# The low parts of all weight blocks: a negated copy on ScalarE and an accumulating DMA in place of a VectorE subtract

## The chip, the cores and the metric

The kernel runs on one core of a Trainium2 chip. The metric is device time in microseconds. Engines are named as the profile names them: PE is TensorE's matrix multiply and PEld its weight load, DVE is VectorE, ACT is ScalarE, POOL is GpSimd, SP is SyncE, which issues DMAs. Each engine works through a queue of its own in order; a semaphore holds an instruction back until what it needs is there, and everything behind it in that queue waits too.

## The reference

Four layers of width 1024 over 1024 positions, with the token mixers convolution, state space, RWKV-7 and convolution again. All is float32. Cut to what matters:

```python
for i in range(DEPTH):                      # DEPTH = 4
    kind, j = i % N_MIXERS, i // N_MIXERS   # 0 conv, 1 S5, 2 RWKV-7
    ...                                     # y = mixer(x), its products with conv_w_in, ssm_w_in, rwkv_w_rkvz, ..._w_out
    r = DN_ALPHA * x + y
    r = r + (p[i] @ ple_proj[i]) * jax.nn.sigmoid(r @ ple_gate[i])
    x = layer_norm(r, ln_g[i], ln_b[i])
```

The convolution's mixer is `(bg * conv * silu(z)) @ w_out` with `bg, cg, h, z` the four quarters of `x @ w_in`. Nearly all arithmetic is in products of activations with weight matrices.

## The kernel before

**Products from hi and lo parts.** A float32 product is made of three products of operands in a second format, fp32r. Every operand is split: hi is the value rounded to fp32r, lo is the value less hi. `mm3` (L317) adds hi x hi (L326), hi weight x lo activation (L327) and lo weight x hi activation (L328) in PSUM. So each block of weights is needed as two tiles, `wh` and `wl`.

**Blocks of weights.** A block is 128 columns of a matrix, held as 128 partitions x 8 x 128 values (512 KB). `wload` (L290) loads it into a raw tile `wraw` by a DMA of SyncE (L295), rounds it into `wh` on ScalarE (L298) and writes `wl = wraw - wh` on VectorE (L299). Each of the three tiles has three buffers, and `w_fill` loads two blocks ahead (AHEAD = 2) of the one in use, in the order of `weight_order`. So the split of a block can begin only when TensorE has finished with the block that held its buffers, and must be done when TensorE comes to it. A block of one 512-column half is used by 24 products (8 depths x 3); in some stages both halves use it, 48 products.

**Stages.** In the gate stages (`gate_half`, L908) each of eight blocks of `ple_gate` is used by 24 products (tile `gp`), followed by 6 products with a block of `ple_proj` (tile `pp`), which stays for four of them and holds one of the three buffers meanwhile. GpSimd sums r (L920) and the row sums for the layer norm (`ln_s`, L905) there. The RWKV layer mixes products with many small steps on VectorE, ScalarE and GpSimd. The last layer's convolution (`conv_quads`, from L484) computes two by two blocks of the product by a scheme with seven products in place of eight: `w_quad` (L440) loads two raw blocks r0 and r1 (L446, L447), forms sums c1 and c3 of them on VectorE (L465, L466, L472) and r1 in place (L473), and splits c1, c3, r1 and in some quads r0 by its helper `hilo` (L456 on ScalarE, L457 on VectorE). c1 and c3 have one buffer each, and the tiles of c3's split (`w3h`, `w3l`) too. TensorE's order in a quad is the product of c1 with t6 (tile `qa`), the two products of the quad before that use its r1 (`qa`, `qc`), c1 with t5 (`qc`), and c3 with t7 (`qa`). So c1 of the next quad can be split when r1 of the quad before has been used, and two products of 12 instructions each lie between that and its first use.

**Order.** The code is written as a program in which a scheduler places each engine's instructions by its own costs and the tiles' dependencies; what stands in each queue is shown below where it matters.

Of the kernel before, what the change touches and what calls it, by code (L numbers as in the profile page):

```python
# [11 lines left out]
AF = mybir.ActivationFunctionType  # L12
ALU = mybir.AluOpType
# [18 lines left out]
def f32(ap):  # L32
    return ap.bitcast(F32)
# [256 lines left out]
def wload(S, spec):  # L290
    nc = S.nc
    name, idx, c0, kt, n = spec
    W = S.A[name][idx]
    raw = S.wp.tile([P, kt, n], F32, tag="wraw", name="wraw", bufs=3)
    nc.sync.dma_start(raw, W.rearrange("(k p) n -> p k n", p=P)[:, :, c0:c0 + n])  # L295
    wh = S.wp.tile([P, kt, n], F32R, tag="wh", name="wh", bufs=3)
    wl = S.wp.tile([P, kt, n], F32R, tag="wl", name="wl", bufs=3)
    nc.scalar.copy(wh, raw)  # L298
    nc.vector.tensor_tensor(wl, raw, f32(wh[:]), ALU.subtract)  # L299
    return wh, wl  # L300


def wprep(S, name, idx, c0, kt=8, n=P):
# [7 lines left out]
def w_fill(S):  # L311

    while len(S.wready) < min(1 + AHEAD, len(S.worder)) and S.worder[len(S.wready)]:
        S.wready.append(wload(S, S.worder[len(S.wready)]))
# [125 lines left out]
def w_quad(S, name, idx, c0, full):  # L440

    nc = S.nc
    V = nc.vector
    W = S.A[name][idx].rearrange("(k p) n -> p k n", p=P)
    r0, r1 = (S.wp.tile([P, NB, P], F32, tag="wraw", name="wraw", bufs=3) for _ in range(2))
    nc.sync.dma_start(r1, W[:, :, c0 + HT:c0 + HT + P])  # L446
    nc.sync.dma_start(r0, W[:, :, c0:c0 + P])  # L447
    yield
    q = {}

    def hilo(src, k=NB):
        if k == NB:
            wh, wl = (S.wp.tile([P, k, P], F32R, tag=t, name=t, bufs=3) for t in ("wh", "wl"))
        else:
            wh, wl = (S.ws.tile([P, k, P], F32R, tag=t, name=t, bufs=1) for t in ("w3h", "w3l"))
        nc.scalar.copy(wh, src)  # L456
        V.tensor_tensor(wl, src, f32(wh[:]), ALU.subtract)  # L457
        return wh, wl

    if full:  # L460
        w = hilo(r0)
        q[1], q[2] = (*w, 0), (*w, 4)
        yield
    c1 = S.ws.tile([P, NB, P], F32, tag="c1", name="c1", bufs=1)
    V.tensor_tensor(c1[:, 4:8, :], r1[:, 0:4, :], r1[:, 4:8, :], ALU.add)  # L465
    V.tensor_tensor(c1[:, 0:4, :], c1[:, 4:8, :], r0[:, 0:4, :], ALU.add)  # L466
    yield
    w = hilo(c1)
    q[6], q[5] = (*w, 0), (*w, 4)
    yield  # L470
    c3 = S.ws.tile([P, 4, P], F32, tag="c3", name="c3", bufs=1)
    V.tensor_tensor(c3, r0[:, 0:4, :], r1[:, 0:4, :], ALU.add)  # L472
    V.tensor_tensor(r1[:, 0:4, :], c1[:, 0:4, :], r0[:, 4:8, :], ALU.add)  # L473
    yield
    w = hilo(c3, 4)
    q[7] = (*w, 0)
    yield
    w = hilo(r1)
    q[3], q[4] = (*w, 0), (*w, 4)
    S.wq.append(q)  # L480
    yield
# [1724 lines left out]
```

## Time and profile before

| | |
|---|---|
| median of 3 runs | 2836.13 us (2835.7 to 2843.77) |
| the profiled execution | 2839.38 us, of which the span is 2837.7 us |
| mean granted TensorE clock | 0.963 of full speed |
| moved by DMA | 331.56 MB, all but 2.6 MB of it through SyncE's queue; DMA engines 38.3% busy |
| blocks split | 307: L298/L299 255 times, L456/L457 52 times |

The profile is one execution. It gives for each group of instructions the busy time, the mean duration and the idle time of the engine just before, with what ended that. The chain of waits goes back from the last instruction to what released each, so it shows what set the end. TensorE's products overlap in their pipeline: the record of one is 0.39 us long, but the next starts 0.23 us after it. DMA issues are not counted as busy time of an engine.

### The profile page before, as it was taken

How to read it: one execution, taken by the hardware profiler on the slowest of the kernel's cores; microseconds unless marked ns; L12 is line 12 of the kernel's file. 1: busy time of each engine (PE TensorE's matmuls, PEld its weight loads, DVE VectorE, ACT ScalarE, POOL GpSimd, SP SyncE). 2: the span in 40 equal slices, each digit the busy share in tenths (PEclk: the TensorE clock that was granted, in tenths of full speed). 3: DMA queues.
4: the chain of work that ended last, by engine and by line, in shares of the span. 5: the costliest groups of instructions: out<-in, count | busy, mean ns of one | idle time of the engine just before them, and what ended most of it. 6: DMA issues, size and time to landing. Idle time of an engine off the chain costs nothing.

```text
span 2837.7 us, 40655 instructions
## 1 busy us (share of the span) xinstructions
PE 2681.3 (94%) x14939; PEld 2127.4 (75%) x14939; DVE 1994.8 (70%) x3584; ACT 1163.1 (41%) x2211; POOL 646.9 (23%) x696
## 2 busy tenths in 40 slices
PE   8999999999999999899888799898889999999998
PEld 6877788778877888576667567666768777887887
DVE  6787865477657346888888667888756678876544
ACT  3333322242135223656555476555534343224332
POOL 1143422221116132203333110333232211111000
PEclk9999999999999999999997799999699999999999
DMA  5333322347884333473222245223234433324511
GB/s 168 98 97 97 95 75 66 89 142 212 220 240 140 104 94 122 117 233 107 78 85 87 63 151 170 84 91 89 78 100 135 144 111 111 108 71 129 171 64 38
DMA packets 463128, 331.56 MB, mean 117 GB/s; under 512 B 49449, under 2 KB 398929, under 8 KB 462929
## 3 DMA queue, kind: packets, MB, share of 16 engines
q1 hardware_dynamic: 462928, 328.96, 38.3%
q8 instruction: 118, 1.93, 0.3%
q14 instruction: 82, 0.66, 0.1%
HBM read 250.77 MB, written 77.59 MB: 116 GB/s over the span
## 4 chain that ended last, share of the span: by engine, by line
PE 70%; DVE 16%; ACT 4%; issue 4%; DMA 3%; POOL 3%; SPq 0%; DVEq 0%; POOLq 0%; ACTq 0%
PE op L327 3%; PE op L326 3%; PE op L328 3%; PE gp L328 3%; PE gp L327 3%; PE gp L326 3%; PE sp L326 3%; PE sp L327 3%; PE sp L328 2%; DVE tv L2048 2%; PE qa L508 2%; PE qa L506 2%; PE qa L507 2%; PE zp L326 2%; PE zp L328 2%
## 5 line engine op out<-in xcount | busy, mean ns | idle before, releaser
L299 DVE TENSOR_TENSOR wl<-wraw,wh 128x1024 fp32r<-128x1024 f32 x255 | 331.1, 1299 | 217.9 <-ACT wh L298 214.2
L298 ACT CAST wh<-wraw 128x1024 fp32r<-128x1024 f32 x255 | 267.5, 1049 | 517.7 <-PE gp L327 191.5
L905 POOL TENSOR_TENSOR ln_s<-ln_s,rp 128x512 f32<-128x512 f32 x42 | 60.0, 1429 | 209.8 <-DVE rp L901 209.8
L2134 DVE SCALAR_TENSOR_TENSOR state<-state,pc,p 64x64 f32<-64x64 f32 x256 | 71.1, 278 | 46.9 <-PE p L2131 42.1
L2048 DVE TENSOR_TENSOR tv<-ti,mi 128x128 f32<-128x128 f32 (+3 forms) x128 | 97.8, 764 | 2.4
L2127 PE MATMUL p<-state,ra 128*128 128x128 f32 x256 | 65.6, 343 | 28.8 <-DVE state L2134 26.7
L2128 ACT COPY uv<-p 64x128 f32<-64x128 f32 x128 | 33.1, 259 | 136.5 <-PE p L2127 135.8
L2127 PEld LDWEIGHTS p<-state,ra 128*128 128x128 f32 x256 | 45.8, 217 | 54.1 <-DVE state L2134 44.0
L1982 PEld LDWEIGHTS s<-ra,kb 64*128 64x128 f32 x512 | 64.7, 213 | 20.4 <-ACT scr L1988 6.2
L1982 PE MATMUL s<-ra,kb 64*128 64x128 f32 x512 | 75.2, 314 | 4.1 <-DVE kb L1738 1.9
L328 PE MATMUL gp<-r_0h,wl 128*128 128x512 f32 x192 | 77.5, 404 | 0.0
L327 PE MATMUL gp<-r_0l,wh 128*128 128x512 f32 x192 | 76.8, 400 | 0.0
L326 PE MATMUL gp<-r_0h,wh 128*128 128x512 f32 x192 | 76.6, 399 | 0.0
L326 PE MATMUL gp<-r_1h,wh 128*128 128x512 f32 x192 | 76.4, 398 | 0.0
L920 POOL TENSOR_TENSOR rp<-r_0h,r_0l 128x512 f32<-128x512 f32 x24 | 36.3, 1544 | 174.9 <-PE op L327 174.9
L328 PE MATMUL gp<-r_1h,wl 128*128 128x512 f32 x192 | 76.1, 396 | 0.1
L2131 PE MATMUL p<-uv,kbt 128*128 128x128 f32 x256 | 66.8, 347 | 9.9 <-ACT uv L2128 9.8
L327 PE MATMUL gp<-r_1l,wh 128*128 128x512 f32 x192 | 75.6, 394 | 0.0
L2131 PEld LDWEIGHTS p<-uv,kbt 128*128 128x128 f32 x256 | 44.5, 212 | 37.7 <-ACT uv L2128 31.9
L1991 POOL TENSOR_TENSOR scr<-scr,mask 128x512 f32<-128x512 f32 x32 | 46.0, 1436 | 55.4 <-ACT scr L1988 55.2
L326 PE MATMUL sp<-xs0h,wh 128*128 128x512 f32 x128 | 56.1, 438 | 2.6 <-DVE aq L1720 2.2
L327 PE MATMUL sp<-xs0l,wh 128*128 128x512 f32 x128 | 56.0, 437 | 1.9 <-DVE xs0l L195 1.9
(851 smaller groups left out, 8669.6 us busy)
## 6 DMA issues: line engine op xcount, KB each, us to landing
wraw<-in_conv_w_in_dram SPq DMA_DIRECT2D x84, 512.0 KB
wraw<-in_rwkv_w_rkvz_dram SPq DMA_DIRECT2D x64, 512.0 KB
wraw<-in_ple_gate_dram SPq DMA_DIRECT2D x56, 512.0 KB
wraw<-in_conv_w_out_dram SPq DMA_DIRECT2D x24, 512.0 KB
xt<-xd SPq DMA_DIRECT2D x48, 256.0 KB
wraw<-in_ssm_w_in_dram SPq DMA_DIRECT2D x21, 512.0 KB
xd<-rp SPq DMA_DIRECT2D x40, 256.0 KB
wraw<-in_rwkv_w_out_dram SPq DMA_DIRECT2D x16, 512.0 KB
```

Source lines behind the costliest of these rows:

```text
L298: nc.scalar.copy(wh, raw)
L299: nc.vector.tensor_tensor(wl, raw, f32(wh[:]), ALU.subtract)
L326: nc.tensor.matmul(ps, lh, xh, start=(n == 0), stop=False)
L327: nc.tensor.matmul(ps, lh, xl, start=False, stop=False)
L328: nc.tensor.matmul(ps, ll, xh, start=False, stop=(n == kt - 1))
L506: nc.tensor.matmul(ps, wh[:, k0 + k, :], xh, start=first and k == 0, stop=False, skip_group_check=True)
L905: nc.gpsimd.tensor_tensor(s, s, rs, ALU.add)
L1982: nc.tensor.matmul(pss[hd][:, c * P:(c + 1) * P], kb[rows, 2 * c + w, :], ra[rows, 2 * c + w, :], start=True, stop=True)
L2048: V.tensor_tensor(tv, ti[:, b:8, 4 * b:4 * b + 4].unsqueeze(2).to_broadcast([P, n, c, 4]), mi[:, 4 * b:4 * b + 4, 0:c].rearrange("p q c -> ...
L2127: nc.tensor.matmul(p1, R.ra[:, c, :], st, start=False, stop=False, skip_group_check=True)
L2131: last = nc.tensor.matmul(p2[:, 0:P], R.kbt[c // 4][:, c % 4, :], uv, start=True, stop=True)
L2134: V.scalar_tensor_tensor(st[cs, cs], st[cs, cs], R.pc[cs, c:c + 1], p2[cs, cs], ALU.mult, ALU.add)
```

## The change

In both places where a block of weights is split, VectorE's subtract goes. ScalarE writes a second tile, the raw values times -1, rounded to fp32r, which is -hi, into `wl`; then a DMA issued by GpSimd adds the raw block to it in place (`accum_op=ALU.add`), from SBUF to SBUF, 512 KB (256 KB for c3). What `wl` holds then is raw - hi, as before.

```diff
@@ -295,9 +295,16 @@
     nc.sync.dma_start(raw, W.rearrange("(k p) n -> p k n", p=P)[:, :, c0:c0 + n])
     wh = S.wp.tile([P, kt, n], F32R, tag="wh", name="wh", bufs=3)
     wl = S.wp.tile([P, kt, n], F32R, tag="wl", name="wl", bufs=3)
-    nc.scalar.copy(wh, raw)
-    nc.vector.tensor_tensor(wl, raw, f32(wh[:]), ALU.subtract)
+    split_added(S, (wh, wl), raw)
     return wh, wl
+
+
+def split_added(S, hl, src):
+
+    hi, lo = hl
+    S.nc.scalar.copy(hi, src)
+    S.nc.scalar.activation(lo, src, AF.Copy, scale=-1.0)
+    S.nc.gpsimd.dma_start(f32(lo[:]), src, accum_op=ALU.add)
 
 
 def wprep(S, name, idx, c0, kt=8, n=P):
@@ -453,8 +460,7 @@
             wh, wl = (S.wp.tile([P, k, P], F32R, tag=t, name=t, bufs=3) for t in ("wh", "wl"))
         else:
             wh, wl = (S.ws.tile([P, k, P], F32R, tag=t, name=t, bufs=1) for t in ("w3h", "w3l"))
-        nc.scalar.copy(wh, src)
-        V.tensor_tensor(wl, src, f32(wh[:]), ALU.subtract)
+        split_added(S, (wh, wl), src)
         return wh, wl
 
     if full:
```

Lines behind the new function stand six or seven further down in the changed kernel. The scheduler also gives each engine a new order. ScalarE in the quads of the last layer, before: the splits of one quad's c1, r1 (`wraw`) and c3, between sigmoids.

```order
L541 ACTIVATE sg_22411<-s1_21349 128x512
L456 CAST wh_22394<-c1_22391 128x1024
L541 ACTIVATE sg_22428<-s2_22269 128x512
L456 CAST wh_22469<-wraw_22371 128x1024
L456 CAST w3h_22448<-c3_22432 128x512
```

The same place in the changed program:

```order
L547 ACTIVATE sg_22248<-s1_21358 128x512
L305 CAST wh_22230<-c1_22227 128x1024
L306 ACTIVATE wl_22231<-c1_22227 128x1024
L547 ACTIVATE sg_22265<-s2_22104 128x512
L305 CAST wh_22307<-wraw_22209 128x1024
L306 ACTIVATE wl_22308<-wraw_22209 128x1024
L305 CAST w3h_22285<-c3_22269 128x512
L306 ACTIVATE w3l_22286<-c3_22269 128x512
```

Each negated copy stands right behind its cast. GpSimd at that place, before: only the products of the convolution with the gate, and copies of the columns that one half hands to the next.

```order
L543 TENSOR_TENSOR cv_21376<-cv_21376,sg_21424 128x512
L534 COPY car_21583<-u_21580 128x2
L543 TENSOR_TENSOR cv_21585<-cv_21585,sg_21635 128x512
L534 COPY car_21883<-u_21880 128x2
L530 COPY u_21889<-car_21883 128x2
```

GpSimd there in the changed program, with the accumulating DMAs of c1, r1 and c3 of two quads:

```order
L307 DMA wl_22204<-wraw_22088 128x1024
L307 DMA w3l_22180<-c3_22163 128x512
L549 TENSOR_TENSOR cv_22139<-cv_22139,sg_22199 128x512
L549 TENSOR_TENSOR cv_22132<-cv_22132,sg_22248 128x512
L307 DMA wl_22231<-c1_22227 128x1024
L549 TENSOR_TENSOR cv_22159<-cv_22159,sg_22265 128x512
L307 DMA wl_22308<-wraw_22209 128x1024
L307 DMA w3l_22286<-c3_22269 128x512
```

The DMAs stand between GpSimd's own work, three to a quad. VectorE's additions into c1 and c3 of the next quad now wait for the landing of the DMA that reads the present ones.

TensorE at the start of the gate stage of the S5 layer, where a new block of `ple_proj` has just come, before:

```order
L328 MATMUL pp_8989<-pT1_8789,wl_8627 128x512
L326 MATMUL gp_9015<-r0_0h_8227,wh_8960 128x512
L327 MATMUL gp_9015<-r0_0l_8228,wh_8960 128x512
L326 MATMUL pp_9040<-pT0_8781,wh_8915 128x512
L327 MATMUL pp_9040<-pT0_8781,wh_8915 128x512
L328 MATMUL gp_9015<-r0_0h_8227,wl_8961 128x512
```

The same place in the changed program, from the middle of the products that now stand between gp's two products with wh and its first with wl:

```order
L333 MATMUL pp_9154<-pT1_8896,wh_9025 128x512
L334 MATMUL pp_9154<-pT1_8896,wh_9025 128x512
L335 MATMUL pp_9154<-pT1_8896,wl_9026 128x512
L333 MATMUL gp_9175<-r0_0h_8327,wh_9117 128x512
L334 MATMUL gp_9175<-r0_0l_8328,wh_9117 128x512
L333 MATMUL pp_9200<-pT0_8888,wh_9025 128x512
L334 MATMUL pp_9200<-pT0_8888,wh_9025 128x512
L335 MATMUL pp_9200<-pT0_8888,wl_9026 128x512
L333 MATMUL pp_9200<-pT1_8896,wh_9025 128x512
L334 MATMUL pp_9200<-pT1_8896,wh_9025 128x512
L335 MATMUL pp_9200<-pT1_8896,wl_9026 128x512
L335 MATMUL gp_9129<-r0_0h_8327,wl_9072 128x512
```

Two products with `pp` stood ahead of the first `gp` with `wl` before; now all products of `pp` for two blocks and the first two of the next `gp` do. The number of products is the same.

## The prediction

> **What bounds the kernel now.** I read the page first, for the share of each engine.
>
> ```profile
> PE 2681.3 (94%) x14939; PEld 2127.4 (75%) x14939; DVE 1994.8 (70%) x3584; ACT 1163.1 (41%) x2211; POOL 646.9 (23%) x696
> PE 70%; DVE 16%; ACT 4%; issue 4%; DMA 3%; POOL 3%; SPq 0%; DVEq 0%; POOLq 0%; ACTq 0%
> ```
>
> TensorE is busy for 2681.3 of 2837.7 us and carries 70% of the chain that ended last. Idle time of TensorE is 156 us in all, and no relief of another engine can give more than that. The busy times by stretch show where it lies.
>
> ```profile
> 1206.00:2128.00 922.00, 821.17 (x6416) 632.04 (x6416) 716.66 (x1507) 509.43 (x1229) 241.60 (x240) 0.90 0.35 109
> 2128.00:2290.00 162.00, 159.16 (x697) 128.12 (x697) 100.06 (x134) 58.04 (x80) 39.01 (x28) 1.00 0.43 133
> 2290.00:2602.00 312.00, 307.06 (x1313) 247.72 (x1312) 250.31 (x354) 110.03 (x152) 41.49 (x41) 0.98 0.33 98
> ```
>
> The columns are the stretch, its length, then busy time of PE, PEld, DVE, ACT and POOL, the clock, the DMA share and GB/s. In the RWKV layer (first row) TensorE is idle for 101 of 922 us, with VectorE busy for 717. In a gate stage (second row) and in the last layer's quads (third row) it is idle for 3 and 5 us: there any block of weights that comes late is paid in full.
>
> **What goes.** All 307 subtracts leave VectorE. The groups by line give their sizes.
>
> ```profile
> L299 DVE TENSOR_TENSOR wl<-wraw,wh 128x1024 fp32r<-128x1024 f32 x255 | 331.1, 1299 | 217.9 <-ACT wh L298 214.2 <-PE mu L960 2.7
> L298 ACT CAST wh<-wraw 128x1024 fp32r<-128x1024 f32 x255 | 267.5, 1049 | 517.7 <-PE gp L327 191.5 <-issue 77.4 <-PE op L327 67.2
> L457 DVE TENSOR_TENSOR wl<-wraw,wh 128x1024 fp32r<-128x1024 f32 x20 | 25.0, 1248 | 1.8 <-ACT wh L456 1.5
> L457 DVE TENSOR_TENSOR wl<-c,wh 128x1024 fp32r<-128x1024 f32 x16 | 21.5, 1345 | 8.1 <-ACT wh L456 7.9
> L457 DVE TENSOR_TENSOR w3l<-c,w3h 128x512 fp32r<-128x512 f32 x16 | 11.0, 685 | 2.9 <-ACT w3h L456 2.9
> ```
>
> VectorE loses 331.1 + 25.0 + 21.5 + 11.0 = 389 us of work, and the 218 us in which its queue stood still at L299 until ScalarE had written wh. That is not the gain: most of it lies beside TensorE. The chain of waits, gone through in full, holds 49 pieces of such subtracts, 45.3 us together, and 17 pieces of the casts, 17.6 us; the first and the last of each are
>
> ```profile
> 15.53 1.06 ACT wh L298
> 16.61 1.24 DVE wl L299
> ...
> 2357.62 0.86 DVE wl L457
> ...
> 2615.19 1.06 ACT wh L298
> ```
>
> 45 us is the most that their going gives by this chain. Sixteen of the 49 (17 us) lie in RWKV, where TensorE does idle; many others lie where it is always busy, and there the next chain is as long. I take half: **-22 us**.
>
> **What comes on ScalarE.** 307 negated copies. The trace has no such instruction; the cast of the same 128x1024 tile, 1049 ns, is the nearest, and I take it: 307 x 1.05, less half for the sixteen 128x512 tiles, is 314 us. ScalarE goes from 1163 to about 1480 us of 2837, far from a bound. A second copy behind each of the 17.6 us of casts on the chain could cost 18 us at most and nothing at least; half, **+9 us**.
>
> **What comes on GpSimd and the DMA queues.** 307 accumulating DMAs wait for the negated copy in GpSimd's in-order queue, where the work of 647 us stands. Behind them wait the sums of the gate (L905) and RWKV steps that TensorE waits for:
>
> ```profile
> POOL ln_s L905 <- DVE rp L901: 209.8, 42, 6.8
> PEld otp L2169 <- POOL o L2162: 18.0, 11, 7.2
> PEld kbtp L2006 <- POOL kb L2001: 15.9, 11, 2.5
> ```
>
> The sums have idle time before them (210 us in 42 waits, 5 us each), which hides a DMA issue. The other two are 34 us of direct waits; if a DMA stands before a seventh of such steps they grow by **+5 us**; nothing at least, 15 at most. SyncE is touched too:
>
> ```profile
> SPq L295 <- DVE wl L299: 770.4, 168, 12.5
> ```
>
> Its loads wait until the raw tile is released, which was the subtract's end and is now the landing of the accumulate, some 5 us later. A raw tile is used again three blocks on (17 us at one product a block), and a load takes 4.5 us (below), so the next load still ends before its cast; I cost this at nothing. If that cover were gone, each block would be late by what is missing.
>
> **The term that decides: when wl is there.** The rows below are from the timeline of a quad, the release of a weight buffer first, then the cast that waited for it, the subtract, and the first products that use the block.
>
> ```profile
> 2451.26 0.39 PE L508 MATMUL qc<-b22h,wl 128*128 128x512 f32 x1
> ...
> 2451.59 1.04 ACT L456 CAST wh<-c 128x1024 fp32r<-128x1024 f32 x1
> ...
> 2453.10 1.22 DVE L457 TENSOR_TENSOR wl<-c,wh 128x1024 fp32r<-128x1024 f32 x1
> ...
> 2457.04 0.40 PE L506 MATMUL qa<-t6h,wh 128*128 128x512 f32 x1
> ...
> 2457.50 0.39 PE L508 MATMUL qa<-t6h,wl 128*128 128x512 f32 x1
> ```
>
> TensorE starts a product every 0.23 us. Between the release (2451.5) and the first use of wl (2457.5) stand 26 products, **6.0 us**. The old path needed 1.05 + 1.22 and small gaps. The new one needs 1.05 (hi) + 1.05 (negated) + L, with L the time from there to the landed sum, so the stall is L - 3.9. In the order of the changed program 23 blocks have such a window of 26 to 28 products. Gate stages have narrower ones:
>
> ```profile
> 1058.04 0.39 PE L328 MATMUL gp<-r_0h,wl 128*128 128x512 f32 x1
> ...
> 1058.24 1.05 ACT L298 CAST wh<-wraw 128x1024 fp32r<-128x1024 f32 x1 [5.25 <-PE gp L327]
> ...
> 1059.33 1.22 DVE L299 TENSOR_TENSOR wl<-wraw,wh 128x1024 fp32r<-128x1024 f32 x1 [4.17 <-ACT wh L298]
> ...
> 1059.63 0.39 PE L326 MATMUL gp<-r_0h,wh 128*128 128x512 f32 x1
> ...
> 1060.61 0.50 PE L328 MATMUL gp<-r_0h,wl 128*128 128x512 f32 x1
> ```
>
> Here only 11 products (2.5 us) lay between, just enough. The new order puts other products (pp) ahead of the first gp with wl, and widens such windows to 16 to 24 products, 4.9 us in the mean over 12 blocks: stall L - 2.8. Another 15 have 30 to 32 products, 7.1 us: L - 5.0. All others have 34 or more, most of RWKV far more. The first block of all waits, but so do the loads behind it, and I cost it at nothing.
>
> L is not in the trace; no DMA there is issued by GpSimd or accumulates. The nearest rows are a block's load and a transfer from SBUF to SBUF, both pieces of the chain (from issue to landing), and one load in steps of 1 us (it was issued at 2442.71):
>
> ```profile
> 1175.02 4.64 DMA lhl<-lo
> ...
> 2341.80 4.51 DMA wraw<-in_conv_w_in_dram
> ```
> ```profile
> 2442.71 0.37 SPq L446 DMA_DIRECT2D wraw<-in_conv_w_in_dram  x1
> ```
> ```profile
> 2443.00:2444.00 1.00, 1.00 (x6) 0.83 (x5) 0.67 (x2) 0.62 (x1) 0.00 (x0) 1.00 0.11 33
> 2444.00:2445.00 1.00, 1.00 (x6) 0.78 (x6) 1.00 (x3) 0.00 (x0) 0.00 (x0) 1.00 0.74 175
> 2445.00:2446.00 1.00, 1.00 (x6) 0.82 (x5) 1.00 (x3) 0.00 (x0) 0.00 (x0) 1.00 1.00 300
> ```
>
> About 1.1 us pass before data, 2 us carry the 512 KB, and 1.3 us pass before it counts as landed. A sum reads a second operand: 2 us more gives 6.5. Low end 3.4 (the load without the last wait), high end 9.3 (twice the 4.64). I take 5.2, near the two rows of 4.5 and 4.6 with a part of a second read.
>
> The Trainium skill, DMA: Bandwidth & Descriptors, section "Anatomy of one DMA — SWDGE (gpsimd) path", gives about 2.0 us plus bytes at 436 GB/s for such a DMA: an estimate from it is 3.2 us for 512 KB, and the sum would be the first rival's; it speaks of plain transfers, and no run here shows one yet.
>
> At 5.2 the stalls are 23 x 1.3 + 12 x 2.4 + 15 x 0.2 = 30 + 29 + 3 = **+62 us**. The sum is 62 - 22 + 9 + 5 = +54 us on 2839.4 us, the profiled execution's own time (span 2837.7). Against the median of the runs, 2836.1, that is **2890 us**.
>
> **Rivals.** *Hidden, and VectorE's relief pays* (faster): L is 3.9 or less, so that the 23 windows hold, the 12 cost 12 us or less, and the relief gives 30 us with ScalarE and GpSimd costing little: 2836 - 30 + 10, about 2816. For it: VectorE is 78% busy in RWKV. Against: TensorE idles for 101 us there, and VectorE's queue is only one of what it waits for. It turns at L = 4.0, where stalls and gain cancel; between 4.0 and 4.3 the result is within the 0.3% that a measurement can tell from no change. *The accumulate is slow* (L about 7.8, the sum passing through DMA engines that also carry the loads, 35 to 43% busy above): 23 x 3.9 + 12 x 5.0 + 15 x 2.8 = 192, with some 20 us of windows of 34 to 40 products, gives 2836 + 212 - 8, about 3040. *GpSimd's queue holds the DMAs up*: a DMA that comes behind one sum of the gate waits up to 6.8 us; if half of the 27 narrower gate windows lose 3 us, 40 us come on top: 2930.
>
> The Trainium skill, SBUF — State Buffer, section "Reading the diagram" with its box on the trap of SWDGE, says that GpSimd cannot write descriptors while VectorE runs an instruction in a two-port mode. An estimate: with VectorE's usual 0.69 us here, L grows by at most that, 24 us over the first 35 windows, about 2914; whether these instructions use that mode no run shows.
>
> **How the numbers follow.** Forecast (stalls of wl beat the relief) 0.46; GpSimd's queue on top 0.09; slow accumulate 0.13; hidden and faster 0.20; L near the turn 0.12. Range: the low end is the faster rival with L at 3.4, about 2812; the high end takes in the slow rival, 3040, and leaves out L up to 9.3 (some 3130) and a larger relief. Faster by over 0.3%: 0.20; within 0.3%: 0.12; slower: 0.68.
>
> **What would show it.** Right: VectorE about 1605 us busy and ScalarE about 1480; TensorE waiting for a DMA of wl in the quads by 1 to 2 us each, some 23 times, and more at the gates' first blocks; the stretch 2290 to 2602 longer by 25 us; RWKV shorter by 10 to 20. Wrong: no waits for wl in the quads (L under 3.9), or waits of 3 us and more in all gate blocks.

## The result and the profile after

| | before | after |
|---|---|---|
| median of 4 runs, us | 2836.7 | 3040.2 (3034.7 to 3048.2) |
| ratio, 95% interval | | 1.071 [1.068, 1.074] |
| span of the profiled execution, us | 2837.7 | 3038.4 |
| mean granted TensorE clock | 0.963 | 0.945 |
| busy share of the DMA engines, two queues | 38.3% | 35.9% + 27.8% |

The change costs 204 us, where 54 were forecast; the time lies at the high end of the range, to which the rival of the slow accumulate had led. The first lines of the page of the changed kernel (engines' busy time, then the two DMA queues: packets, MB, share of the 16 engines' span):

```profile
PE 2749.6 (90%) x14939; PEld 2163.4 (71%) x14939; DVE 1675.9 (55%) x3277; ACT 1442.3 (47%) x2518; POOL 855.5 (28%) x1003
q1 hardware_dynamic: 462928, 328.96, 35.9%
q0 software_dynamic: 44208, 156.78, 27.8%
```

VectorE has fallen from 70% to 55% and TensorE's idle time has risen from 156 to 289 us. TensorE is also busy for 68 us more with the same products, so some of them ran slower (below). The new queue moves 157 MB in 27.8% of the span, the old one 329 MB in 35.9%: a byte of the sum costs 1.6 times the engines' time of a byte of the rest.

The groups of the split by line (count | busy, mean ns of one | idle before):

```profile
L305 ACT CAST wh<-wraw 128x1024 fp32r<-128x1024 f32 x275 | 288.2, 1048 | 523.5 <-issue 152.1
L307 POOL DMA_DIRECT2D wl<-wraw x275 | 239.3, 871 | 1054.7 <-ACT wl L306 958.7
L306 ACT ACTIVATE wl<-wraw 128x1024 fp32r<-128x1024 f32 x275 | 290.4, 1056 | 1.6 <-PE sp L335 1.4
```

The negated copy takes 1.056 us, as assumed. Its DMA keeps GpSimd for 0.87 us each time. The view of line 307 ends with the time from issue to landing:

```profile
DMA to landing us min/median/max: 4.3/5.4/9.7
```

What TensorE waited for, from the waits of the changed kernel (total, times, longest):

```profile
PE gp L335 <- DMA wl<-wraw: 33.6, 16, 5.5
PE ppt L878 <- DMA praw<-in_p_dram: 19.4, 7, 4.9
PE op L335 <- DMA wl<-wraw: 16.1, 6, 5.4
PE qa L514 <- DMA wl<-c: 12.9, 12, 2.6
PE q L514 <- DMA wl<-wraw: 11.1, 8, 3.6
PE zp L335 <- DMA wl<-wraw: 7.6, 2, 5.6
PE up L335 <- DMA wl<-wraw: 7.0, 3, 4.4
```

Waits for wl, of which there were none before, come to 98 us in all rows of this view; counted block by block, from one product's start to the next less the usual 0.23 us, 55 blocks lose 108 us. The waits for the rows of p that a gate loads (praw) come to 19.4 us, before to 4.1. Not all of that is the DMA engines. In the first gate, where 8.5 of the 19.4 lie, two waits of 6.2 us together are for rows whose loads SyncE issues only from 506.4 us on: it had waited since 501.4 for one subtract of VectorE, r_0l. That takes 11.3 us here (0.69 is the median of the 32), beside sums of r that stand back to back on GpSimd:

```profile
495.08 11.27 DVE L195 TENSOR_TENSOR r_0l<-r,r_0h 128x512 fp32r<-128x512 f32 x1 [0.69 <-ACT r_0h L195]
...
498.14 7.65 POOL L926 TENSOR_TENSOR rp<-r_1h,r_1l 128x512 f32<-128x512 f32 x6
...
514.53 0.69 PE L878 MATMUL ppt<-ident,praw 128*128 128x128 f32 x2 [4.79 <-DMA praw<-in_p_dram]
```

The second gate has one such subtract of 9.1 us. The run with the plain copy has both too (11.0 and 8.9 us); the kernel before and the runs in which VectorE makes the gates' low parts have none over 2 us there. Why it is so slow was not tried.

**By stage.** A stage ends with the same product in each trace; times in us. The three runs beside before and after are explained with the experiments.

| stage (time before) | before | VectorE adds | plain copy | sum (after) | copies beside |
|---|---|---|---|---|---|
| start (0 to 100) | 100 | 100 | 108 | 113 | 115 |
| first convolution (to 487) | 387 | 387 | 384 | 385 | 414 |
| gate 1 (to 610) | 123 | 121 | 136 | 142 | 124 |
| S5, first part (to 820) | 210 | 210 | 218 | 242 | 239 |
| S5, second part (to 1030) | 210 | 212 | 211 | 221 | 220 |
| gate 2 (to 1145) | 115 | 114 | 128 | 146 | 118 |
| RWKV (to 2128) | 983 | 1008 | 973 | 994 | 1025 |
| gate 3 (to 2290) | 162 | 175 | 177 | 196 | 179 |
| quads (to 2602) | 312 | 310 | 308 | 342 | 325 |
| the rest | 234 | 235 | 245 | 256 | 241 |

The windows behind some of these (stretch, its length, busy time of PE, PEld, DVE, ACT and POOL, clock, DMA share, GB/s). First before: S5's first part and the second gate. Then after: the same two, most of RWKV, the third gate, the quads, and the start of the last layer's conv_w_out.

```profile
610.00:820.00 210.00, 207.25 (x1203) 170.90 (x1202) 147.09 (x198) 54.67 (x81) 35.95 (x52) 0.99 0.78 212
1030.00:1145.00 115.00, 113.70 (x512) 92.73 (x511) 75.64 (x104) 40.92 (x59) 35.66 (x34) 1.00 0.36 109
```
```profile
640.00:882.00 242.00, 215.85 (x1204) 177.71 (x1203) 122.78 (x176) 70.91 (x98) 51.39 (x71) 0.95 0.87 225
1103.00:1249.00 146.00, 127.60 (x510) 101.14 (x511) 59.45 (x87) 58.71 (x78) 49.62 (x52) 0.91 0.67 159
1416.00:2243.00 827.00, 731.75 (x6010) 560.29 (x6009) 589.54 (x1330) 502.30 (x1190) 272.80 (x290) 0.90 0.50 133
2243.00:2439.00 196.00, 168.86 (x691) 132.71 (x690) 66.46 (x106) 84.46 (x108) 59.81 (x56) 0.94 0.74 181
2439.00:2781.00 342.00, 313.42 (x1314) 246.62 (x1312) 188.77 (x292) 162.45 (x216) 85.92 (x103) 0.99 0.77 173
2781.00:2866.00 85.00, 78.65 (x339) 62.77 (x340) 28.54 (x43) 37.93 (x52) 10.35 (x12) 0.98 0.90 232
```

The clock is the second thing to see. In the second gate it falls from 1.00 to 0.91, and the same products take 127.6 us in place of 113.7. The timeline there shows how: a product, a wait of 3.49 us, and then products that start every 0.43 us until 5.6 us after the wait's end, when the pace of 0.23 returns.

```profile
1139.87 0.39 PE L335 MATMUL pp<-pT,wl 128*128 128x512 f32 x1
1143.74 0.79 PE L335 MATMUL gp<-r_0h,wl 128*128 128x512 f32 x1 [3.49 <-DMA wl<-wraw]
1144.33 0.63 PE L333 MATMUL gp<-r_0h,wh 128*128 128x512 f32 x1
1144.76 0.63 PE L334 MATMUL gp<-r_0l,wh 128*128 128x512 f32 x1
...
1149.37 0.40 PE L333 MATMUL gp<-r_0h,wh 128*128 128x512 f32 x1
1149.60 0.40 PE L334 MATMUL gp<-r_0l,wh 128*128 128x512 f32 x1
```

Weight products that start 0.40 to 0.48 us after the one before number 81 in the trace of before and 253 after; over 0.23 us each they cost 16 and 50 us. So 34 of the 204 us are a slow clock behind the waits, not waits; the rest of the 68 us was not traced.

### The profile page after: what moved, and what is told of

Its sections match the earlier page's. It is cut to its first block, busy times and chain, and to the rows that moved or that the text cites. A ratio compares the mean times of both kernels' runs of the same rounds, so it can differ in the third digit from the quotient of the medians.

```text
span 3038.4 us, 41475 instructions
## 1 busy us (share of the span) xinstructions
PE 2749.6 (90%) x14939; PEld 2163.4 (71%) x14939; DVE 1675.9 (55%) x3277; ACT 1442.3 (47%) x2518; POOL 855.5 (28%) x1003
## 3 DMA queue, kind: packets, MB, share of 16 engines
q1 hardware_dynamic: 462928, 328.96, 35.9%
q0 software_dynamic: 44208, 156.78, 27.8%
q8 instruction: 118, 1.93, 0.3%
## 5 line engine op out<-in xcount | busy, mean ns | idle before, releaser
L305 ACT CAST wh<-wraw 128x1024 fp32r<-128x1024 f32 x275 | 288.2, 1048 | 523.5 <-issue 152.1
L307 POOL DMA_DIRECT2D wl<-wraw x275 | 239.3, 871 | 1054.7 <-ACT wl L306 958.7
L306 ACT ACTIVATE wl<-wraw 128x1024 fp32r<-128x1024 f32 x275 | 290.4, 1056 | 1.6 <-PE sp L335 1.4
L906 DVE TENSOR_TENSOR sg<-pp,sg 128x512 f32<-128x512 f32 x48 | 33.2, 691 | 230.5 <-ACT sg L905 230.5
L335 PE MATMUL op<-y_1h,wl 128*128 128x512 f32 x128 | 52.1, 407 | 12.3 <-DMA wl<-wraw 12.3
```

Of the source, the lines that this page charges most:

```text
L305: S.nc.scalar.copy(hi, src)
L306: S.nc.scalar.activation(lo, src, AF.Copy, scale=-1.0)
L307: S.nc.gpsimd.dma_start(f32(lo[:]), src, accum_op=ALU.add)
L335: nc.tensor.matmul(ps, ll, xh, start=False, stop=(n == kt - 1))
```

## The experiments

The theories at the start: W or L, TensorE waits for the late landing of wl; E, ScalarE's and GpSimd's queues hold others up; T, the DMA engines' time by itself slows everything that is transferred. H, the ring of raw blocks, and C, the clock, came up on the way. All edits are to the changed kernel unless said otherwise; each time is a median, with the ratio to the kernel before.

**ScalarE alone (VectorE adds).**

```diff
-    S.nc.gpsimd.dma_start(f32(lo[:]), src, accum_op=ALU.add)
+    S.nc.vector.tensor_tensor(lo, src, f32(lo[:]), ALU.add)
```

> ScalarE's negated copy stays, VectorE adds the raw block to it (in place), no DMA from GpSimd. Theory W (TensorE waits for the landing of wl, in the changed kernel 55 blocks and 108 us by its trace, and its clock is slow for some products behind each longer wait): without the landing about 5 us per block go, and what stays is ScalarE's second copy, 1.05 us more before wl: 2836 to 2875, no wait of TensorE for wl over 2 us. Rival E (the second copy in ScalarE's queue holds up the gates' sigmoids and the casts; VectorE waits 230 us for them in the changed kernel): stays above 2900. Rival T (the transfers themselves slow loads and the raw blocks' release): also near 2836 to 2860 here, told apart by a run with the transfers alone.

2875.3 against 2837.3 before (ratio 1.013 [1.011, 1.016]), no wait for wl. It lies at the upper bound of W's range, and E, which had it above 2900, falls. ScalarE's second copy, with the low part that it delays, costs 38 us, and the table shows where: 25 in RWKV and 13 in the third gate, next to nothing elsewhere.

**A plain copy in the sum's place.**

```diff
-    S.nc.gpsimd.dma_start(f32(lo[:]), src, accum_op=ALU.add)
+    S.nc.gpsimd.dma_start(f32(lo[:]), src)
```

> The DMA from GpSimd copies the raw block over the negated copy and does not add (the low part is then the whole weight, so this part of the computation is changed). Prediction's working took 2 us more for a second operand. If a sum lands later than a copy by that much: landing 3.4 us where the sum's lowest is 4.3, stalls of some 55 fewer us, about 2960. If the sum costs nothing more: landing 4.3 to 4.5 at the low end, 3040 +- 15.

What `wl` holds is then the whole weight. 2890.8 (1.018 [1.016, 1.021]), far below the 2960 that was expected for a copy that lands sooner. The same bytes, issued from the same place, but its page and its line 307 read

```profile
q0 software_dynamic: 43184, 156.78, 14.2%
```
```profile
DMA to landing us min/median/max: 2.3/3.4/8.3
```

14.2% of 2889.8 us is 410 us of all 16 engines; 27.8% of 3038.4 is 845. **The sum costs the DMA engines 2.06 times a copy's time, and lands 2.0 us later.** The sum in the copy's place is 149 of the 204 us, and besides these two only the issue on GpSimd is longer, 0.87 us in place of 0.56. The Trainium skill, Collectives: The Full Stack, section "The bandwidth ceiling: the fold count and why AG ≠ RS ≠ AR", says for collectives that a reducing transfer is slower not by the add but by reading two sources, one descriptor each on the same ring, and gives 1.93 as the measured ratio of the two bandwidths. The trace here agrees in size, with its 2.06; that the second read is the reason no run here shows. The estimate that the prediction made of 3.2 us by the Trainium skill, DMA: Bandwidth & Descriptors, section "Anatomy of one DMA — SWDGE (gpsimd) path", fits the plain copy's 3.4, not the sum's 5.4; the section names no accumulate.

**A delay without transfers, and transfers without a delay.**

```diff
+    part = lo[:, 0:src.shape[1] * 3 // 4, :]
+    S.nc.gpsimd.tensor_scalar(part, f32(part), 1.0, None, ALU.mult)
     S.nc.gpsimd.dma_start(f32(lo[:]), src)
```

> The plain copy (2891 us; the sum in its place 3040), with a pass of GpSimd over three quarters of the negated block ahead of each copy; as in the plain copy, the low part is then the whole weight. By the page's 1.38 us for 512 columns it holds each copy up by some 2.1 us, so that wl lands as late as the sum's (5.9 us after the negated copy's end against 6.1), while the DMA engines carry what they carry for the copy. Theory L (the 149 us are the later landing alone): 2980 to 3040. Theory T (they are the DMA engines' time, which the sum doubles from 14% to 28% of the span): 2930 or less. Between: both.

```diff
     S.nc.gpsimd.dma_start(f32(lo[:]), src)
+    d = S.dram.tile(list(src.shape), F32, tag="spare", name="spare", bufs=4)
+    S.nc.gpsimd.dma_start(d, src)
```

> The plain copy, and behind each a second one of the raw block to a scratch in HBM that nobody reads (the low part is the whole weight, as in the plain copy). The DMA engines then have about the time of the sum to carry, and the raw block is held as long, but wl's own copy goes first. Theory T: 2980 to 3040, with TensorE's waits on wh, p's rows and the loads rather than on wl. Theory L: 2930 or less.

3054.2 and 3073.2 (1.077 and 1.083): both lose more than the 149 us, so the totals do not tell the theories apart, and the expectation that one of the two would stay near 2891 was wrong. TensorE's waits for wl rise from 24 us to 105 and to 85. Neither run is clean: the first nearly doubles GpSimd's busy time (762 to 1407 us), and in the second wl's copy lands later too (4.1 us in the median by its page, against 3.5). So a third one keeps wl out of it: VectorE adds, and two copies to HBM run beside.

```diff
-    S.nc.gpsimd.dma_start(f32(lo[:]), src, accum_op=ALU.add)
+    S.nc.vector.tensor_tensor(lo, src, f32(lo[:]), ALU.add)
+    for _ in range(2):
+        d = S.dram.tile(list(src.shape), F32, tag="spare", name="spare", bufs=4)
+        S.nc.gpsimd.dma_start(d, src)
```

> The kernel with VectorE's add (2875 us; no wait of TensorE for wl), and behind it two plain copies of each raw block from GpSimd to a scratch in HBM. The DMA engines carry about what the sums cost them, but wl does not wait for them. Theory T (the DMA engines' time by itself, and the raw block's later release with it): 2960 or more. Theory L (only the landing of wl matters): 2870 to 2900.

2999.1 (1.055 [1.051, 1.058]): 124 us by transfers with wl out of it (GpSimd's issues and the raw block's later release come with them), on engines as busy as with the sum:

```profile
q0 software_dynamic: 86368, 313.56, 28.2%
```

The last column of the table above tells more than the total. These transfers cost S5's first part and the start what the sum costs there (239 against 242 us, 115 against 113), but only 3 to 4 us more than their own base in each gate, where the sum costs 21 to 32. They write to HBM, unlike the sum, and cost the first convolution 27 us that the sum does not; so the total is no measure of the sum's share, but the stages part.

**The sum taken out of one stage.**

```diff
-    split_added(S, (wh, wl), raw)
+    if name.startswith("ple"):
+        nc.scalar.copy(wh, raw)
+        nc.vector.tensor_tensor(wl, raw, f32(wh[:]), ALU.subtract)
+    else:
+        split_added(S, (wh, wl), raw)
```

> The changed kernel, with the 70 blocks of the gate (ple_gate, ple_proj) split by VectorE as before and all others by the sum. Theory L in the gates (narrow windows, the landing of wl ends the wait; with twice the copies' traffic and wl on time these stages lost only 3 to 4 us each): the three gate stages, 21, 32 and 35 us longer in the changed kernel, go back to within 5 to 10 us of before: 2955 to 2985. Theory T there: 3010 or more.

2970.0 (1.046 [1.045, 1.048]), and the second gate is back at 115 us with the clock at 1.00:

```profile
1077.00:1192.00 115.00, 113.80 (x512) 92.74 (x512) 74.33 (x103) 41.70 (x60) 36.28 (x36) 1.00 0.37 108
```

The three gates take 122, 115 and 171 us, against 142, 146 and 196: the 70 us that the whole run gained are theirs. The slow subtracts of r_0l are gone with it, so the first gate's part is not the landing's alone. The same with `"ssm"` in place of `"ple"`:

> The changed kernel, with the 37 blocks of the S5 layer split by VectorE as before. Theory T in S5 (its own transfers keep the DMA engines 78% busy before, and the sums' time does not fit): the stretch of 210 us before that takes 242 us goes back to under 220, 43 us or nearly that in all: 2995 to 3010. If the loss there came from elsewhere (the clock, ScalarE): 3025 or more.

2996.7 (1.055 [1.052, 1.057]), 44 us less, and S5's two parts are back at 212 and 211 us:

```profile
641.00:853.00 212.00, 207.53 (x1206) 171.49 (x1205) 148.65 (x200) 54.88 (x81) 36.67 (x52) 0.99 0.77 212
```

Both expectations held. The gates lose to the landing: transfers without it cost them 3 to 4 us. S5 loses to the transfers: without a late wl they cost it as much as the sum, on engines that its own transfers keep 78% busy before the change. That the landing adds nothing there is not shown; with the delayed copy, S5's first part takes 232 us where the plain copy's takes 218, but GpSimd's extra work is in that too.

**wl later in each block.**

```diff
         nc.tensor.matmul(ps, lh, xl, start=False, stop=False)
-        nc.tensor.matmul(ps, ll, xh, start=False, stop=(n == kt - 1))
...
+    for n, k in enumerate(ks or range(kt)):
+        nc.tensor.matmul(ps, wl[:, k, ms:ms + P], rhs[k][0], start=False, stop=(n == kt - 1))
```

> The changed kernel with the products of each block put in another order: all products with wh first, those with wl last. The first use of wl comes 16 products (3.7 us) later in a block of 24, 8 (1.8 us) later in a quad's block of 12. Theory W: by the windows of this program's order and 6 us for the landing, stalls of some 40 us in place of 108, and two thirds of the slow clock behind them gone: about 2950 (2900 to 2985). Rivals E and T: nothing they name is touched, at most 20 us faster, 3020 or more.

> The kernel before with the same order of products. Control: its wl is there in time for nearly all blocks, so every theory says 2825 to 2845. If this order costs or gains by itself, the run of the changed kernel in this order is to be read against it.

3039.2 and 2861.8. In its total the first is a miss for W: the waits for wl fell from 98 to 29 us, as its windows said, and the time did not move. TensorE waits 21 us more for ScalarE and 20 us more for VectorE; ScalarE's casts wait 115 us for loads (72 in the changed kernel, 27 before); and the order costs 25 us by itself, which the control did not expect either. By stage it is less of a miss. The second gate, the third and the quads take 127, 185 and 331 us in place of 146, 196 and 342, as W says. S5's first part, where the transfers count, takes 239 in place of 242. S5's second part and RWKV take 12 and 24 us more, and the control puts 9 and 16 of these on the order. Its chain of waits and that of the changed kernel suggested a ring: load, two passes of ScalarE, sum, and the next load only behind the landing. The chain of the changed kernel reads near its end, in its longest pieces:

```profile
2844.14 5.42 DMA wraw<-in_ple_gate_dram
2850.73 0.95 ACT wh L305
2851.68 0.96 ACT wl L306
2852.93 7.81 DMA wl<-wraw
2860.79 5.34 DMA wraw<-in_ple_gate_dram
```

**Four raw blocks.** There is room only with fewer work tiles, so a control has those alone. All tiles with the tag wraw get a fourth buffer, of which one is shown.

```diff
-NTS = (7, 7, 8)
+NTS = (5, 5, 6)
...
-    raw = S.wp.tile([P, kt, n], F32, tag="wraw", name="wraw", bufs=3)
+    raw = S.wp.tile([P, kt, n], F32, tag="wraw", name="wraw", bufs=4)
```

> Control for the next two: the changed kernel with two fewer of the small work tiles (7, 7 and 8 become 5, 5 and 6), which makes room for one more raw block. Fewer work tiles can only hold something up: 3040 to 3080.

> The changed kernel with four raw blocks in place of three (and two fewer work tiles, as in the control). Theory H (a raw block is released by the sum's landing, so that load, the two passes of ScalarE and the sum turn in a ring of some 16 us for three blocks, which the chain of waits of the changed kernel shows at its end: 5.4 + 1.0 + 1.0 + 7.8): the casts' waits for loads (72 us, 24 times) go to under 30 us, and 30 to 80 us against the control. Theory W (the wait for wl at its own use): within 15 us of the control.

> Four raw blocks and the products with wl last in each block. If the landing and the raw ring are two limits at the same height, so that the order alone (3039 us) gained nothing because the ring took over: 2950 to 3000, clearly below both. If the DMA engines' time is the limit: 3020 or more, as with either.

3083.4, 3081.6 and 3096.7; the control lies just above its range. The casts' waits for loads fall (67 to 45 us, and to 26 with wl last), and nothing is gained; S5's first part takes 238 us, the control 241. H falls: the ring on the chain is not what sets the time, and the raw block's later release is not what S5 loses. That load and sum share engines that are 90% busy there remains the likelier reason, not tried by itself.

**Two half sums.**

```diff
+    m = src.shape[1] // 2
+    for k in (slice(0, m), slice(m, 2 * m)):
+        S.nc.scalar.activation(lo[:, k, :], src[:, k, :], AF.Copy, scale=-1.0)
+        S.nc.gpsimd.dma_start(f32(lo[:, k, :]), src[:, k, :], accum_op=ALU.add)
```

> The changed kernel with the negated copy and the sum of each block in two halves, the first half's sum issued before the second half's copy. The first half starts 0.5 us earlier and carries half: by the copy's and the load's rows (2 us to carry 512 KB) and twice that for a sum, it lands some 2 us sooner after its issue. Theory L: the waits at the first wl product fall by 1.5 to 2.5 us each, some 60 us in all, against 267 us more of GpSimd's issuing: 2980 to 3020. Theory T (DMA time unchanged) or GpSimd's queue: 3040 or more.

3063.1 (1.078 [1.073, 1.082]). Half a block lands after 4.8 us in the median where the whole takes 5.4, not the 2 us sooner that were expected. But the two halves run side by side, the second issued some 0.6 us behind the first: the first halves of the 275 blocks from `wraw` land after 4.3 us, the second after 5.4. The quickest half takes 3.3 us and the quickest whole 4.5. TensorE waits 58 us for wl in place of 98 and loses that elsewhere, with GpSimd issuing twice as often at the same 0.88 us:

```profile
DMA to landing us min/median/max: 3.3/4.8/10.3
```

**The clock.** A product by zeros fills the wait, at six blocks of the gates.

```diff
+FILL = {21: 8, 23: 8, 31: 14, 37: 8, 41: 14, 45: 8}
...
+        for _ in range(fill if n == 0 else 0):
+            nc.tensor.matmul(ps[0:16, :], S.zero16, xh, start=False, stop=False)
```

> The changed kernel, with 8 or 14 products by a weight of zeros (16 columns) ahead of the first wl product of six blocks at the gates that wait 3.5 to 5.7 us in its trace (the 21st, 23rd, 31st, 37th, 41st and 45th). They fill 1.8 to 3.2 us of each wait and change no sum. Theory C (behind a wait of over about 2.8 us, 7 to 13 products take 0.43 us in place of 0.23): those six waits fall to 1.5 to 2.5 us, and the products behind them start every 0.23 us: 6 x 2.1 = 13 us less, 3027. Rival: the slow products are the price of the contention itself: 0.43 us stay behind these waits, 3040 +- 5.

3031.3 (1.069 [1.066, 1.072]); the 9 us less lie inside the two intervals, but the timeline shows the mechanism at all six places. The same wait as above, 3.04 us of it left:

```profile
1138.09 0.39 PE L342 MATMUL gp<-r_0l,wh 128*128 128x512 f32 x1
1141.52 0.50 PE L345 MATMUL gp<-r_0h,wl 128*128 128x512 f32 x1 [3.04 <-DMA wl<-wraw]
1141.85 0.39 PE L341 MATMUL gp<-r_0h,wh 128*128 128x512 f32 x1
1142.08 0.40 PE L342 MATMUL gp<-r_0l,wh 128*128 128x512 f32 x1
```

From the second on, every product behind it starts 0.23 us after the last. C holds for these six. The Trainium skill, TensorE: Matmul & The Clock Gate, section "What's actually happening", states that the clock halves after an idle window of about 3.4 us and returns after as long a busy one; the trace agrees, with 0.43 against 0.23 us behind every wait of 3.29 us and more at a weight product, and not behind this one of 3.04 (a few shorter waits close upon others slow it too). The return is less regular here: the pace of 0.23 was back 3.2 to 7.1 us after such a wait's end in the changed kernel.

**What VectorE's relief is worth.** The kernel before, with the RWKV projections' subtracts on GpSimd:

```diff
-    nc.vector.tensor_tensor(wl, raw, f32(wh[:]), ALU.subtract)
+    e = nc.gpsimd if name == "rwkv_w_rkvz" else nc.vector
+    e.tensor_tensor(wl, raw, f32(wh[:]), ALU.subtract)
```

> The kernel before, with the subtracts of the RWKV blocks (64 loads of them in rwkv_w_rkvz) on GpSimd in VectorE's place. By the two runs that differ in VectorE's add alone, its work is worth some 32 us in the RWKV layer (853 against 821 us there), and here ScalarE has nothing more to do. If that relief is real by itself: 2805 to 2828. If GpSimd's longer subtract (some 2.75 us by its 1.38 for half of it) holds up its queue or comes late: 2836 or more.

2885.9 (1.017 [1.015, 1.019]), all of the 48 us in RWKV; GpSimd takes 2.40 us for a subtract, where 2.75 had been estimated, but its place in the queue or the later wl costs more than VectorE gains (which of them was not tried). And the changed kernel with the sum at 88 blocks only (the quads' blocks, whose code is not shown, are VectorE's again too):

```diff
-    split_added(S, (wh, wl), raw)
+    if name == "rwkv_w_rkvz" or name == "conv_w_in" and idx == (0,) and c0 % D >= 2 * P:
+        split_added(S, (wh, wl), raw)
+    else:
+        nc.scalar.copy(wh, raw)
+        nc.vector.tensor_tensor(wl, raw, f32(wh[:]), ALU.subtract)
```

> A version: the sum only for 88 blocks with windows wide enough by the traces (RWKV's four projections and the first layer's conv_w_in from the third column block on), VectorE for all others, quads too. These two stretches took 385 and 827 us in the changed kernel and 387 and 828 before, so no gain is in sight by the sum of stages: 2830 to 2850, the same within 0.3%. If VectorE's relief pays once nothing is late around it: 2825 or less.

2843.0 against 2837.7 (1.002 [1.001, 1.004]): where the sum comes in time, nothing is gained by it. No version here beats the kernel before.

## Why the prediction was wrong

**What bounds the kernel** held: TensorE had 156 us to give, and stages in which it never waits paid each late block in full.

**VectorE's relief, -22 us.** It exists where it was placed: between the runs in which VectorE adds and in which a copy does it, RWKV goes from 1008 to 973 us, 35 less. But VectorE is busy for 1676 us and not 1605. Its records overlap, so that without the subtracts the trace of before has it busy for 1639; the two slow subtracts of r_0l are 19 of the 37 us that came on top. And RWKV in the changed kernel is not 10 to 20 us shorter, as the signs had it, but 11 longer.

**ScalarE, +9 us,** was too small: +38 by the run with VectorE's add. Half of the casts on the chain of before says nothing of the work behind them: that in RWKV ScalarE's other steps stand behind the second copy is the likely reason, not tried by itself. Together, relief and second copy are about nothing, as the 88 blocks show.

**GpSimd, +5 us,** was no cost in its own work: TensorE's direct waits for GpSimd fell from 39.6 to 19.0 us, and the sums of the gate wait less than the 210 us of before:

```profile
POOL ln_s L911 <- DVE rp L907: 40.7, 38, 4.0
```

The rival of its queue holding the DMAs up is seen at four of the 55 late blocks, issued 2.3 to 9.1 us after the negated copy's end; most follow by 0.3 us.

**The raw block's later release, cost at nothing:** casts wait 72 us for loads in place of 27, but a fourth block did not pay, so the term is small by itself.

**The late low part, +62 us.** The mechanism was right: a wait of TensorE at the first product with wl, by what the path from release to landing has over the window. Its size was not: 55 waits lose 108 us. By its own windows, with the median L of all blocks from `wraw` or c1, 6.1 us from the negated copy's end to the landing, 23 x 2.2 + 12 x 3.3 + 15 x 1.1 = 107. That this meets 108 is luck, for by place it does not fit: the quads lost 30 us, the gates 37 and all else 41. In the quads the forecast sum came out, 23 waits and 30 us, where 23 x 1.3 = 30 were forecast, though the single waits there run from 0.3 to 3.8 us; the stretch is 30 us longer, not 25. A quad's wait, with the cast that follows the release, the negated copy, the DMA and the first use:

```profile
2588.70 1.05 ACT L305 CAST wh<-c 128x1024 fp32r<-128x1024 f32 x1 [8.07 <-PE qc L513]
...
2589.66 1.05 ACT L306 ACTIVATE wl<-c 128x1024 fp32r<-128x1024 f32 x1
...
2591.00 0.85 POOL L307 DMA_DIRECT2D wl<-c  x1 [9.23 <-ACT wl L306]
...
2595.93 0.49 PE L514 MATMUL qa<-t6h,wl 128*128 128x512 f32 x1 [1.02 <-DMA wl<-c]
```

**The step that failed is one L for all stages.** 5.2 us was near what the quads' late blocks have, 5.6 in the mean and 4.9 in the median from the negated copy's end; at the gates the mean is 6.7, elsewhere 8.2. In S5 and the last layer's conv_w_out the DMA engines are 87 and 90% busy (the rows above), and the blocks that wait there land 5.8 to 9.4 us after issue. Outside quads and gates there are 16 waits of 41 us, where 3 us at most were forecast, and at the gates 16 of 37 us, where the 12 narrowest windows were to cost 29. That the sum takes 2.06 copies' worth of engine time was not in the working at all; its "part of a second read" was put on the landing, never on the engines that loads, p's rows and S5's transfers share.

**Two terms were missing.** The slow clock behind long waits, 34 us. And other waits that grew: for p's rows, 15 us more, some 6 of it in the first gate behind the slow subtract, and at S5's products with its own transferred operands 11 us, before 1; for half of the latter the view names a transfer, for the other half nothing:

```profile
PE s5s L1358 <- DMA s_ba<-s_bad: 5.5, 3, 2.9
PE s5s L1358 <- issue: 5.3, 1, 5.3
```

The sum in runs: ScalarE's copy +38, the DMA as a plain copy in place of VectorE's add +16, the sum in place of the copy +149. The rival of the slow accumulate named the cause, engines that also carry the loads, and the time, but by an L of 7.8 everywhere, where the median is 6.1 and TensorE's waits for wl are 108 us, not its 212; that its 3040 us came out is luck too, as the clock and other waits made up the rest. The terms found here, 108 + 34 + 15 + 10 us, make 167 of the 204; the other 37 are not put down to any one cause. Open is also how the 149 us split between landing and engine time in the stages where both act (S5, the quads), and what makes S5's second part and RWKV longer with wl last.

## What to carry to other kernels

A DMA that adds is not a copy with a free add: here it took twice the engines' time and 2 us more, so it is to be priced against the busy share of the DMA engines stage by stage, not by one latency. Price a wait of TensorE by its length class: here one of up to 3 us mostly cost itself, a longer one some 2 us more. Where a lead of two blocks is all that memory allows, a step that lengthens the path from load to use is paid in each stage that TensorE fills and whose windows are too narrow for it; the first convolution, with wider ones, paid nothing.

## What the runs showed that was not expected

Half the bytes were worth 1.2 us of a sum's landing at best, 3.3 us in place of 4.5. Its issue keeps GpSimd 0.87 us, against 0.56 for a plain copy of the same block, and 0.88 for half a block. A single VectorE subtract of 0.69 us took 11.3 us beside back-to-back sums on GpSimd. Two fewer work tiles, of seven or eight, cost some 40 us. Putting the products with wl last cost the kernel before 25 us.
